# Attention heads of a hybrid trunk layer: pool waits by tile, two more side blocks ahead of the first value products, query weights converted behind the last head

## The chip, the core and the metric

The kernel runs on one core of a Trainium2 chip. The metric is the device time of one execution in microseconds (us); a kernel is run several times and the median stands for it. The core's engines are TensorE (PE in the profile, its weight loads PEld), VectorE (DVE), ScalarE (ACT), GpSimd (POOL) and SyncE (SP), whose queue issues nearly all DMAs. Each engine takes its instructions in a fixed order and waits on semaphores of the others.

## The reference

One layer of 1024 tokens and width 1024: a mixer of two head groups (forgetting attention, "fox", and gated linear attention), cross-attention to 256 memory tokens, and a squared-ReLU MLP.

```python
def fox_attention(q, k, v, log_f):
    c = jnp.transpose(jnp.cumsum(log_f, axis=1), (0, 2, 1))
    for i in range(S // Q_BLOCK):                      # 8 blocks of 128 queries, keys up to their end
        s = jnp.einsum('bqhd,bkhd->bhqk', qb, kb).astype(jnp.float32) * scale
        s = jnp.where(mask, s + c[:, :, start:end, None] - c[:, :, None, :end], -jnp.inf)
        p = jax.nn.softmax(s, axis=-1)
        outs.append(jnp.einsum('bhqk,bkhd->bqhd', p.astype(vb.dtype), vb))

def parallel_mixer(xn, ...):
    proj = xn @ w_in                                   # both mixers' inputs
    fox_out = fox_attention(rms_norm(fq), rms_norm(fk), fv, log_sigmoid(ff + b))   # 8 heads of 64
    gla_out = rms_norm(gla_chunked(gq, gk, gv, g_log)) * silu(gr)                  # 4 heads
    return concatenate([fox_out, gla_out], axis=-1) @ w_out

def memory_cross_attention(hn, memn, ...):             # 4 heads of 256, 256 memory tokens
    q = rms_norm(hn @ wq); k, v = split(memn @ wkv); k = rms_norm(k)
    return softmax(q k^T / 16) v @ wo

h = x + parallel_mixer(rms_norm(x), ...)
h = h + memory_cross_attention(rms_norm(h), rms_norm(mem), ...)
y = h + relu(rms_norm(h) @ w1)**2 @ w2                 # 1024 -> 4096 -> 1024
```

## The kernel before

All matrices are float32. A large product splits both operands into a rounded high part and a low rest, of type float32r, and makes three matmuls of each pair of tiles (high x high, low x high, high x low): `gemm`, L110 to L112. Every operand so needs a high part from ACT (a copy that rounds: `wh`, `sh`, `pth`) and a low part from DVE (`wl`, `sl`, `ptl`: the source less the high part). `wsplit` (L80 the load `raw`, L88 or L99 the high part, L93 or L100 the low part) does it for weights, `split_half` (L843, L844) for activations, `evac_split` (L117, L118, or L120, L121 with a factor) for what comes out of PSUM.

The stages follow each other: projections and linear attention, then `fox`, `project_out`, cross-attention, `project_o`, and the MLP. This case lies in `fox`, 324 to 548 us after the span's start, and at its end. There are 8 heads. For each, two groups g of four score tiles t (`fox_scores`): PE makes the scores (`s`, L660 to L663, 128 queries x up to 1024 keys), DVE the negated maximum (`nm`, L665), ACT the exponential with its row sum (`p`, L668), DVE the reciprocal (`rrec`, L670) and POOL scales (L671). Scores of more than 512 keys take a wide PSUM tile `s2`, of which there is one, the others an `s1`, also one. `values` then takes two of these tiles at a time (sub-block sb of four): PE transposes (`tr`, L696), ACT and DVE split the result into `pth` and `ptl`, PE multiplies by the values (`pv`, L704, of `va`), ACT copies half of the sum (`ol`, L707), DVE adds the other half (`mixf`, L710). The tiles of the first group of head 0 have their scores made ahead of `fox`. The values reach `va` by way of DRAM: the stage before stores `vd` (L600), `fox` loads it per head (L723).

So that PE has work while the softmax runs, a generator `side_work` gives independent products in blocks: eight blocks of `out_part` 0 (12 matmuls each, the linear attention's share of the mixer's output, `mm`, with `t2k` for the sum with x), then keys and values of the memory (`wkv`, `memr`, 24 matmuls each), then eight blocks of `out_part` 1 (18 each). `step` says after which of the 32 sub-blocks the next block is written:

```python
            def step(s):
                for _ in range(((s + 1) * 26 + 8) // 32 - (s * 26 + 8) // 32):
                    next(side, None)
```

The order in the program is not the order of the code: a scheduler, which works with estimated times of its own, chooses for each engine what comes next among what is ready. `issue_after(x)` holds it: what is issued inside goes behind the instruction x. For heads 6 and 7 the side blocks are held behind the first transposes.

SBUF is given out by pools that are opened and closed like a stack. A new pool over the memory of an old one waits: by default every first use of its tiles waits for all of the old pool's users, with `reuse_waits="tile"` for the users of the memory under that tile alone. `foxpt` holds `pth` and `ptl`, five of each, `foxol` holds `ol`, three. Both lie where the stage before had its tiles, among them those that the stores `vd` read.

Cross-attention converts its query weights (`wq`, `weights(n)`: `wh` L99, `wl` L100) as early as buffers allow, and the first of them are made during the last head.

## Time and profile before

| | |
|---|---|
| median of 3 runs | 1440.09 us (1438.77 to 1441.18) |
| profiled execution | 1440.62 us, its span 1438.9 us |
| PE busy | 1421.3 us, 99% of the span |
| DVE, ACT, POOL busy | 937.8, 675.2, 385.2 us |
| TensorE clock, mean | 0.998 of full |

The times are of runs of the same program; the profile is one execution, 0.53 us above their median. The span runs from its first instruction to its last; 1.7 us of the execution lie outside it. Busy shares are means over stages with different limits, so the prediction reads the stretch in which the change lies.

### The profile page before, as it was taken

The numbers are of one execution on the slowest core, as the hardware profiler recorded it, in microseconds if no ns is written. First come the engines' busy times: TensorE is split into PE (matmuls) and PEld (weight loads), VectorE is DVE, ScalarE is ACT, GpSimd is POOL, SyncE is SP. The second block draws the span as 40 slices with busy tenths as digits, with TensorE's granted clock in tenths as the row PEclk, the third lists the DMA queues.
The fourth block names the chain that finished last, engine by engine and source line by source line (L and its number), as shares of the span: only waits on it lengthen the run. The fifth ranks groups of instructions, "written<-read, shape, count | busy, mean of one in ns | idle before, by whom it ended". The sixth has DMA issues, their size and how long they took to land.

```text
span 1438.9 us, 19147 instructions
## 1 busy us (share of the span) xinstructions
PE 1421.3 (99%) x7036; PEld 1185.4 (82%) x7036; DVE 937.8 (65%) x1342; ACT 675.2 (47%) x1095; POOL 385.2 (27%) x404
## 2 busy tenths in 40 slices
PE   9999999999999999999999999999999999999998
PEld 7788788887888887888888888888888888888887
DVE  5366732437887766666545895656556968778797
ACT  3544441336777655454532364444546745335230
POOL 3235423311333223412212300000000552233454
PEclk9999999999999999999999999999999999999999
DMA  8335530278678634322573124344446835436353
GB/s 313 92 65 140 130 79 0 74 190 285 173 193 239 177 110 148 124 74 90 171 273 140 44 95 179 145 168 190 176 175 231 320 107 190 134 133 217 123 191 124
DMA packets 121164, 223.91 MB, mean 156 GB/s; under 512 B 8912, under 2 KB 54512, under 8 KB 118512
## 3 DMA queue, kind: packets, MB, share of 16 engines
q1 hardware_dynamic: 119776, 218.25, 46.6%
q10 hardware_dynamic: 1296, 4.46, 1.0%
q8 instruction: 55, 0.90, 0.2%
q14 instruction: 37, 0.30, 0.1%
HBM read 150.59 MB, written 72.09 MB: 155 GB/s over the span
## 4 chain that ended last, share of the span: by engine, by line
PE 89%; DMA 4%; ACT 3%; DVE 2%; issue 2%; POOL 0%; SPq 0%; ACTq 0%; DVEq 0%; POOLq 0%
PE mm L110 15%; PE mm L111 15%; PE mm L112 15%; PE my L110 7%; PE my L112 7%; PE my L111 7%; PE tr L112 3%; PE tr L111 3%; PE tr L110 3%; PE pv L704 2%; PE tr L696 2%; PE s L660 1%; PE s L661 1%; DMA ud<-h 1%; DMA raw<-in_mlp_w_dram 1%
## 5 line engine op out<-in xcount | busy, mean ns | idle before, releaser
L110 PE MATMUL my<-x,g 128*128 128x512 f32 x464 | 180.7, 390 | 0.5 <-ACT h L1295 0.3
L111 PE MATMUL my<-x,g 128*128 128x512 f32 x464 | 180.6, 389 | 0.0
L112 PE MATMUL my<-x,g 128*128 128x512 f32 x464 | 180.5, 389 | 0.0
L111 PE MATMUL mm<-wl,xh 128*128 128x512 f32 x320 | 126.5, 396 | 0.6 <-DVE wl L100 0.6
L110 PE MATMUL mm<-wh,xh 128*128 128x512 f32 x320 | 125.9, 396 | 0.5 <-ACT wh L99 0.4
L112 PE MATMUL mm<-wh,xl 128*128 128x512 f32 x320 | 125.7, 393 | 0.0
L1087 ACT ACTIVATE g<-s 128x1024 fp32r<-128x1024 f32 (+1 forms) x72 | 69.0, 964 | 101.1 <-PE my L112 41.1
L1088 DVE TENSOR_TENSOR g<-raw,g 128x512 fp32r<-128x512 f32 (+3 forms) x72 | 69.2, 965 | 69.8 <-ACT g L1087 69.7
L1087 ACT ACTIVATE g<-raw 128x512 fp32r<-128x512 f32 (+3 forms) x72 | 55.5, 773 | 102.4 <-DMA raw<-in_mlp_w_dram 39.6
L110 PEld LDWEIGHTS my<-x,g 128*128 128x128 f32 x464 | 87.1, 188 | 19.5 <-ACT h L1295 0.7
L111 PEld LDWEIGHTS my<-x,g 128*128 128x128 f32 x464 | 87.1, 188 | 18.3 <-DVE x L1088 0.2
L1114 POOL TENSOR_TENSOR s<-raw 128x384 f32<-128x384 f32 (+1 forms) x20 | 26.5, 1324 | 282.1 <-DMA raw<-in_mlp_w_dram 254.5
L112 PEld LDWEIGHTS my<-x,g 128*128 128x128 f32 x464 | 87.1, 188 | 17.9
L671 POOL TENSOR_SCALAR p<-p,rrec 128x128 f32<-128x128 f32 (+3 forms) x64 | 52.8, 831 | 151.6 <-DVE rrec L670 143.1
L1088 DVE TENSOR_TENSOR g<-s,g 128x1024 fp32r<-128x1024 f32 (+1 forms) x72 | 86.6, 1205 | 9.0 <-ACT g L1087 9.0
L1257 DVE TENSOR_TENSOR x<-x 128x1024 fp32r<-128x1024 f32 (+1 forms) x64 | 77.0, 1223 | 17.6 <-ACT x L1256 17.3
L111 PE MATMUL mm<-x,g 128*128 128x512 f32 x220 | 85.7, 389 | 0.0
L110 PE MATMUL mm<-x,g 128*128 128x512 f32 x220 | 85.6, 389 | 0.0
L112 PE MATMUL mm<-x,g 128*128 128x512 f32 x220 | 85.6, 389 | 0.0
L110 PE MATMUL tr<-x,g 128*128 128x512 f32 x212 | 82.5, 389 | 0.0
L111 PE MATMUL tr<-x,g 128*128 128x512 f32 x212 | 82.5, 389 | 0.0
L112 PE MATMUL tr<-x,g 128*128 128x512 f32 x212 | 82.5, 389 | 0.0
(316 smaller groups left out, 3665.8 us busy)
## 6 DMA issues: line engine op xcount, KB each, us to landing
ud<-h SPq DMA_DIRECT2D x32, 768.0 KB
x<-ud SPq DMA_DIRECT2D x48, 512.0 KB
raw<-in_mlp_w_dram SPq DMA_DIRECT2D x20, 1024.0 KB
raw<-in_mlp_w_dram SPq DMA_DIRECT2D x16, 768.0 KB
raw<-in_w_in_dram SPq DMA_DIRECT2D x23, 512.0 KB
raw<-in_xattn_wkv_dram SPq DMA_DIRECT2D x16, 512.0 KB
od<-o SPq DMA_DIRECT2D x32, 256.0 KB
ud<-h SPq DMA_DIRECT2D x32, 256.0 KB
```

The costliest lines, as they stand in the source:

```text
L110: mm(ps, lh[k], rh[k], start=start and k == 0, stop=False, **kw)
L111: mm(ps, lh[k], rl[k], start=False, stop=False, **kw)
L112: mm(ps, ll[k], rh[k], start=False, stop=stop and k == n - 1, **kw)
L660: nc.tensor.matmul(ps[:, c], qa[:, ts], ka[:, c], start=True, stop=False)
L661: nc.tensor.matmul(ps[:, c], qb[0:68, ts], kb[0:68, c], start=False, stop=not last)
L671: nc.gpsimd.tensor_scalar(p[:, 0:n], p[:, 0:n], rr, 1.0, ALU.mult, ALU.mult)
L696: t = nc.tensor.transpose(tp[:, c * P:(c + 1) * P], pp[i][:, (2 * b + j) * P:(2 * b + j + 1) * P], self.ident)
L704: nc.tensor.matmul(pv[:, 256 - (js.stop - js.start):256], va[:, 2 * b + j, :], w[:, js], start=b == j == 0 and w is th, stop=b == sb and j ...
L1087: a = self.nc.scalar.activation(hi, src, AF.Copy)
L1088: d = self.nc.vector.tensor_tensor(lo, src, f(hi), ALU.subtract)
L1114: eng.tensor_tensor(s[:, 0], raw[:, 3], raw[:, 2], ALU.add)
L1257: nc.vector.tensor_tensor(lo, f(lo), f(hi), ALU.subtract)
```

## The change

Three parts. The pool `foxpt` is opened behind `foxol` and waits by tile. Three side blocks are written ahead of the heads instead of one, the steps spread 24 instead of 26 blocks over the sub-blocks, and the first value products (head 0, sub-block 0) are held behind the last matmul of the third side block. The conversions of the query weights are held behind the last head's last two instructions. In the changed kernel the lines of `fox` stand one higher up to the value products and four to six higher behind them.

```diff
     def gemm(...):
...
-            mm(ps, ll[k], rh[k], start=False, stop=stop and k == n - 1, **kw)
+            end = mm(ps, ll[k], rh[k], start=False, stop=stop and k == n - 1, **kw)
+        return end.ins
...
     def fox(self):
-            pt = self.open(st, "foxpt", 5)
             olp = self.open(st, "foxol", 3)
+            pt = self.open(st, "foxpt", 5, reuse_waits="tile")
...
-                    for j, w in ((0, th), (1, th), (1, tl), (0, tl)):
-                        js = slice(j * 256, min((j + 1) * 256, n * P))
-                        nc.tensor.matmul(pv[...], va[:, 2 * b + j, :], w[:, js], ...)
+                    with ExitStack() as behind:
+                        if h == sb == 0:
+                            behind.enter_context(self.tc.issue_after(self.side_end))
+                        for j, w in ((0, th), (1, th), (1, tl), (0, tl)):
+                            js = slice(j * 256, min((j + 1) * 256, n * P))
+                            nc.tensor.matmul(pv[...], va[:, 2 * b + j, :], w[:, js], ...)
...
-                nc.scalar.activation(ol, pv[64:128, :], AF.Copy)
+                end = nc.scalar.activation(ol, pv[64:128, :], AF.Copy).ins
...
-                nc.vector.tensor_tensor(o, v3(pv[0:64, :]), v3(ol), ALU.add)
+                self.fox_end = end, nc.vector.tensor_tensor(o, v3(pv[0:64, :]), v3(ol), ALU.add).ins
...
-            next(side)
+            for _ in range(3):
+                next(side)
...
-                for _ in range(((s + 1) * 26 + 8) // 32 - (s * 26 + 8) // 32):
+                for _ in range(((s + 1) * 24 + 8) // 32 - (s * 24 + 8) // 32):
                     next(side, None)
...
     def out_part(...):
-                self.gemm(ps, *([w[:, c] for w in w_] for w_ in W), *A)
+                self.side_end = self.gemm(ps, *([w[:, c] for w in w_] for w_ in W), *A)
...
             def weights(n):
-                Ws[n] = self.wsplit(self.wq[:, n * 512:(n + 1) * 512], C_XAT)
+                with self.tc.issue_after(self.fox_end[0]), self.tc.issue_after(self.fox_end[1]):
+                    Ws[n] = self.wsplit(self.wq[:, n * 512:(n + 1) * 512], C_XAT)
```

The scheduler makes another order of it. Five places show what the prediction counts on. A number behind a name is that of the tile; the numbers of the two programs differ.

ACT, head 0, first conversions and the exp (`p`) of its last tile, before:

```order
L668 ACTIVATE p_550_2952,rsum_2953<-s_548_2944,nm_2950 128x896 [waits DVE_49]
L117 ACTIVATE pth_2862<-tr_2858 128x384 [waits DMAHW6_49,PE_49,DMAHW7_49,Activation_49,Pool_49]
L117 ACTIVATE pth_2896<-tr_2891 128x512 [waits PE_49]
L117 ACTIVATE pth_2909<-tr_2904 128x512 [waits PE_49]
L668 ACTIVATE p_555_2964,rsum_2965<-s_553_2958,nm_2962 128x512 [waits DVE_49,Pool_49]
L117 ACTIVATE pth_2921<-tr_2917 128x384 [waits PE_49]
L88 ACTIVATE wh_3738<-raw_783_3736 128x512 [waits DMAHW1_49]
L88 ACTIVATE wh_3742<-raw_783_3736 128x512
L88 ACTIVATE wh_3748<-raw_3746 128x512 [waits DMAHW0_49]
L88 ACTIVATE wh_3752<-raw_3746 128x512
L668 ACTIVATE p_560_2978,rsum_2979<-s_558_2970,nm_2976 128x1024 [waits DVE_49,Pool_49]
```

and now:

```order
L669 ACTIVATE p_554_2986,rsum_2987<-s_552_2978,nm_2984 128x896 [waits DVE_49]
L118 ACTIVATE pth_2896<-tr_2892 128x384 [waits PE_49,Activation_49,Pool_49]
L118 ACTIVATE pth_2930<-tr_2925 128x512 [waits PE_49]
L118 ACTIVATE pth_2943<-tr_2938 128x512 [waits PE_49]
L669 ACTIVATE p_559_2998,rsum_2999<-s_557_2992,nm_2996 128x512 [waits DVE_49,Pool_49]
L118 ACTIVATE pth_2955<-tr_2951 128x384 [waits PE_49]
L88 ACTIVATE wh_3683<-raw_769_3681 128x512 [waits DMAHW1_49]
L88 ACTIVATE wh_3687<-raw_769_3681 128x512
L88 ACTIVATE wh_3693<-raw_3691 128x512 [waits DMAHW0_49]
L88 ACTIVATE wh_3697<-raw_3691 128x512
L669 ACTIVATE p_564_3012,rsum_3013<-s_562_3004,nm_3010 128x1024 [waits DVE_49,Pool_49]
```

The row pth_2862, now pth_2896, has lost its two waits on DMAs; the rest keeps its order, with the four wh ahead of the exp.

PE at the same place, from the transposes of head 0 on, before (s_594 is head 1's first wide score):

```order
L696 MATMUL tr_2985<-ident_75,p_555_2964 128x128 [waits Pool_49]
L696 MATMUL tr_2985<-ident_75,p_545_2938 128x128
L696 MATMUL tr_2985<-ident_75,p_555_2964 128x128
L696 MATMUL tr_2998<-ident_75,p_555_2964 128x128 x2
L704 MATMUL pv_2857<-pth_2862,va_2426 128x256 [waits DMAHW7_49,DMAHW6_49,DMAHW3_49]
L704 MATMUL pv_2857<-pth_2862,va_2426 128x128
L704 MATMUL pv_2857<-ptl_2863,va_2426 128x128
L704 MATMUL pv_2857<-ptl_2863,va_2426 128x256
L660 MATMUL s_594_3115<-ka_2848,qa_2846 128x512 [waits Activation_49]
L661 MATMUL s_594_3115<-kb_2849,qb_2847 128x512
```

and now (s_606 is that score):

```order
L697 MATMUL tr_3019<-ident_75,p_559_2998 128x128 [waits Pool_49]
L697 MATMUL tr_3019<-ident_75,p_549_2972 128x128
L697 MATMUL tr_3019<-ident_75,p_559_2998 128x128
L697 MATMUL tr_3032<-ident_75,p_559_2998 128x128 x2
L661 MATMUL s_606_3165<-ka_2882,qa_2880 128x512 [waits Activation_49]
L662 MATMUL s_606_3165<-kb_2883,qb_2881 128x512
L661 MATMUL s_606_3165<-ka_2882,qa_2880 128x256
L662 MATMUL s_606_3165<-kb_2883,qb_2881 128x256
L664 LDWEIGHTS identb_93
L664 MATMUL s_606_3165<-maskb_98,identb_93 128x128
```

The four value products that stood ahead of the score have gone behind it and behind the third side block.

ACT at the fourth side block, before:

```order
L117 ACTIVATE pth_3036<-tr_3031 128x512 [waits PE_49,Activation_49]
L117 ACTIVATE pth_3049<-tr_3044 128x512 [waits PE_49,Activation_49]
L117 ACTIVATE pth_3062<-tr_3057 128x512 [waits PE_49,Activation_49]
L707 ACTIVATE ol_2929<-pv_2890 64x256 [waits PE_49]
L843 ACTIVATE sh_3191<-mixg_120 128x512 [waits PE_49]
L843 ACTIVATE sh_3195<-mixg_120 128x512 [waits PE_49]
L120 ACTIVATE sh_3568<-memr_3576,cols_74 128x256 [waits DMAHW7_49,PE_49]
L120 ACTIVATE sh_3568<-memr_3576,cols_74 128x256
```

and now:

```order
L711 ACTIVATE ol_2904<-pv_2891 64x256 [waits DMAHW7_49,DMAHW6_49,PE_49]
L849 ACTIVATE sh_3055<-mixg_120 128x512 [waits PE_49]
L849 ACTIVATE sh_3059<-mixg_120 128x512 [waits PE_49]
L121 ACTIVATE sh_3445<-memr_3453,cols_74 128x256 [waits DMAHW7_49,PE_49]
L121 ACTIVATE sh_3445<-memr_3453,cols_74 128x256
L121 ACTIVATE sh_3446<-memr_3453,cols_74 128x256 [waits PE_49]
L121 ACTIVATE sh_3446<-memr_3453,cols_74 128x256
L118 ACTIVATE pth_3086<-tr_3081 128x512 [waits PE_49,Activation_49]
L118 ACTIVATE pth_3099<-tr_3094 128x512 [waits PE_49,Activation_49]
L711 ACTIVATE ol_2963<-pv_2924 64x256 [waits PE_49]
```

Two sh and four conversions of memr have moved ahead of pth_3086 and pth_3099.

DVE in the last head (nm_5645 is the maximum of a tile of 1024 keys, rrec_5636 the reciprocal of the tile before it), before:

```order
L118 TENSOR_TENSOR ptl_5568<-tr_5563,pth_5567 128x384 [waits DVE_49,Activation_49]
L670 RECIPROCAL rrec_5636<-rsum_5634 128x1 [waits Activation_49]
L710 TENSOR_TENSOR mixf_2772<-pv_5520,ol_5533 64x2x128 [waits Activation_49]
L817 TENSOR_TENSOR t2k_5597<-mm_5578,t2k_5597 128x512 [waits DMAHW7_49,DMAHW2_49,PE_49]
L665 TENSOR_REDUCE nm_5645<-s_1345_5639 128x1 [waits PE_49]
L670 RECIPROCAL rrec_5650<-rsum_5648 128x1 [waits Activation_49]
```

and now:

```order
L119 TENSOR_TENSOR ptl_5579<-tr_5573,pth_5578 128x512 [waits DVE_49,Activation_49]
L119 TENSOR_TENSOR ptl_5591<-tr_5586,pth_5590 128x384 [waits DVE_49,Activation_49]
L666 TENSOR_REDUCE nm_5645<-s_1345_5639 128x1 [waits PE_49]
L671 RECIPROCAL rrec_5636<-rsum_5634 128x1 [waits Activation_49]
L714 TENSOR_TENSOR mixf_2772<-pv_5559,ol_5598 64x2x128 [waits Activation_49]
L671 RECIPROCAL rrec_5650<-rsum_5648 128x1 [waits Activation_49]
```

The reciprocal has gone behind the wide maximum, and two ptl ahead of it.

DVE behind the last side block, before:

```order
L118 TENSOR_TENSOR ptl_5725<-tr_5719,pth_5724 128x512 [waits DVE_49,Activation_49]
L710 TENSOR_TENSOR mixf_2772<-pv_5653,ol_5679 64x2x128 [waits Activation_49]
L100 SCALAR_TENSOR_TENSOR wl_6155<-raw_6152,cols_74,wh_6154 128x512 [waits DMAHW7_49,Activation_49]
L100 SCALAR_TENSOR_TENSOR wl_6159<-raw_6152,cols_74,wh_6158 128x512 [waits Activation_49]
L118 TENSOR_TENSOR ptl_5738<-tr_5732,pth_5737 128x512 [waits DVE_49,Activation_49]
L118 TENSOR_TENSOR ptl_5750<-tr_5745,pth_5749 128x384 [waits Activation_49]
L844 TENSOR_TENSOR sl_5829<-mixf_2772,sh_5828 128x512 [waits Activation_49]
L844 TENSOR_TENSOR sl_5969<-mixf_2772,sh_5968 128x512 [waits Activation_49]
L844 TENSOR_TENSOR sl_5973<-mixf_2772,sh_5972 128x512 [waits Activation_49]
```

and now:

```order
L119 TENSOR_TENSOR ptl_5725<-tr_5719,pth_5724 128x512 [waits DVE_49,Activation_49]
L119 TENSOR_TENSOR ptl_5738<-tr_5732,pth_5737 128x512 [waits DVE_49,Activation_49]
L850 TENSOR_TENSOR sl_5829<-mixf_2772,sh_5828 128x512 [waits Activation_49]
L850 TENSOR_TENSOR sl_5969<-mixf_2772,sh_5968 128x512 [waits Activation_49]
L850 TENSOR_TENSOR sl_5973<-mixf_2772,sh_5972 128x512 [waits Activation_49]
L119 TENSOR_TENSOR ptl_5750<-tr_5745,pth_5749 128x384 [waits Activation_49]
L714 TENSOR_TENSOR mixf_2772<-pv_5705,ol_5757 64x2x128 [waits Activation_49]
L100 SCALAR_TENSOR_TENSOR wl_6155<-raw_6152,cols_74,wh_6154 128x512 [waits DMAHW7_49,Activation_49]
L100 SCALAR_TENSOR_TENSOR wl_6159<-raw_6152,cols_74,wh_6158 128x512 [waits Activation_49]
```

The two wl of the query weights have gone behind the heads' last rows, and three sl have come ahead of ptl_5750.

More of the change, by code (lines that the diff above doesn't have):

```diff
@@ L701, in values @@
                     self.evac_split(th[:, 0:n * P], tl[:, 0:n * P], tp[:, 0:n * P])
-                    for j, w in ((0, th), (1, th), (1, tl), (0, tl)):
-                        js = slice(j * 256, min((j + 1) * 256, n * P))
-                        nc.tensor.matmul(pv[:, 256 - (js.stop - js.start):256], va[:, 2 * b + j, :], w[:, js],
-                                         start=b == j == 0 and w is th, stop=b == sb and j == 0 and w is tl)
+                    with ExitStack() as behind:
[3 more added lines that the diff above has]
+                            js = slice(j * 256, min((j + 1) * 256, n * P))
+                            nc.tensor.matmul(pv[:, 256 - (js.stop - js.start):256], va[:, 2 * b + j, :], w[:, js],
+                                             start=b == j == 0 and w is th, stop=b == sb and j == 0 and w is tl)
                 ol = self.T(olp, [64, 256], F32, "ol")
-                nc.scalar.activation(ol, pv[64:128, :], AF.Copy)
+                end = nc.scalar.activation(ol, pv[64:128, :], AF.Copy).ins
                 o = self.mixf[(h % 2) * 64:(h % 2) * 64 + 64, 2 * sb:2 * sb + 2, h // 2, :]
                 v3 = lambda ap: ap.rearrange("p (a b) -> p a b", a=2)
-                nc.vector.tensor_tensor(o, v3(pv[0:64, :]), v3(ol), ALU.add)
+                self.fox_end = end, nc.vector.tensor_tensor(o, v3(pv[0:64, :]), v3(ol), ALU.add).ins
                 return first
```

## The prediction

> **What bounds the kernel now.** I read the page's busy shares first, then TensorE's waits over the whole span, then the clock by stretches, then the order of time around the places where the change moves rows.
>
> ```profile
> span 1438.9 us, 19147 instructions
> PE 1421.3 (99%) x7036; PEld 1185.4 (82%) x7036; DVE 937.8 (65%) x1342; ACT 675.2 (47%) x1095; POOL 385.2 (27%) x404
> PE tr L696 <- DVE ptl L118: 4.5, 2, 3.2
> 332.00:336.00 4.00, 1.11 (x4) 0.74 (x5) 1.90 (x4) 2.42 (x6) 0.00 (x0) 0.71 1.04 399
> 336.00:340.00 4.00, 4.00 (x12) 3.23 (x13) 4.00 (x8) 3.02 (x6) 0.69 (x1) 0.50 1.03 387
> 340.00:344.00 4.00, 4.00 (x26) 3.42 (x26) 2.77 (x7) 2.69 (x8) 1.04 (x1) 0.93 1.06 256
> ```
>
> PE is idle for 1438.9 - 1421.3 = 17.6 us in all, so no edit of the order can bring more than that and what half clock costs. The third row is a line of the waits (total, times, longest): one wait of 3.2 us is the longest of the attention heads. The last three rows are stretches of 4 us (behind PE, PEld, ACT, DVE and POOL the sixth figure is the granted clock): 0.71, 0.50, 0.93. At half clock for the shares .29, .50 and .07 doubled, that is 2.3 + 4.0 + .6 = 6.9 us.
>
> ```profile
> 328.41 1.58 SPq L80 DMA_DIRECT2D raw<-in_xattn_wkv_dram  x2
> 330.15 0.67 DVE L665 TENSOR_REDUCE nm<-s 128x1 f32<-128x512 f32 x1
> 331.33 0.23 PE L663 MATMUL s<-maskb,identb 128*128 128x128 bf16 x1
> 333.57 1.47 ACT L117 ACTIVATE pth<-tr 128x384 fp32r<-128x384 f32 x3 [4.31 <-DMA vd<-qn]
> 334.10 1.18 DVE L118 TENSOR_TENSOR ptl<-tr,pth 128x384 fp32r<-128x384 f32 x2 [3.28 <-ACT pth L117]
> 334.80 0.87 PE L696 MATMUL tr<-ident,p 128*128 128x128 f32 x3 [3.24 <-DVE ptl L118]
> 337.18 2.19 ACT L88 ACTIVATE wh<-raw 128x512 fp32r<-128x512 f32 x4 [0.98 <-DMA raw<-in_xattn_wkv_dram]
> 339.27 1.10 ACT L668 ACTIVATE p<-s,nm 128x1024 f32<-128x1024 f32 x1
> 341.24 0.93 PE L696 MATMUL tr<-ident,p 128*128 128x128 f32 x7
> 341.92 0.43 PE L704 MATMUL pv<-pth,va 128*128 128x256 f32 x2
> 342.46 0.40 PE L660 MATMUL s<-ka,qa 128*128 128x512 f32 x1
> 343.57 0.47 PE L110 MATMUL mm<-sh,wh 128*128 128x512 f32 x1
> 346.42 0.49 PE L696 MATMUL tr<-ident,p 128*128 128x128 f32 x3
> ```
>
> These rows are in order of time (start, length). ACT's first conversion of weights (pth) stood idle 4.31 us for the last store of the values (vd), DVE's ptl stood behind it, and PE's next transposes behind ptl: nothing from 331.56 to 334.80. Every one of these tiles comes out of the pool foxpt, which waited for all of the old one.
>
> **Place A, the first head: +0.9 us.** With the pool by tile the order keeps neither wait on the DMA. nm ends at 330.82, pth is done by then, and ptl takes 0.6 (1.18 / 2), so PE goes straight on at 331.56. That frees 3.24 us, and with it the half clock that followed: PE works at half from 334.80 to 340.54, which costs 5.74 / 2 = 2.87.
>
> What is late next: PE does the second side block's rest, a block of 12 matmuls takes 346.42 - 343.57 = 2.85 and seven transposes about 0.7, and is through by 336.3. The next row is the score of head 1, and it needs the wide bank that ACT's exp of head 0's last tile empties. In ACT's order that exp stands behind the four wh, and these behind the load of raw, issued at 328.41, which let the first start at 337.18. Neither changes. So exp runs from 339.27 to 340.37 as before, and PE waits from 336.3 to 340.4, 4.1 us. Before, PE had already more to do there and came to this score at 342.46, when exp was long over. Now it starts it 2.1 earlier, but the first value products (341.92 to 342.46, 0.54) are still owed: 1.5 ahead.
>
> A wait of 3.24 was followed by half clock from 2.15 us after its start, for 6.9 us. Put on a wait that starts at 336.3, this is 338.45 to 345.3, of which PE works 4.9 and loses 2.4. Ends: 0 if the clock holds, 3.0 if the half rate sets in a microsecond later. A wait longer than one that was punished is nearest to that one, so I take 2.4: 2.4 - 1.5 = +0.9, with ends -1.5 and +1.5.
>
> The Trainium skill, "TensorE: Matmul & The Clock Gate", section "Part 1: The HAM clock gate (the "warmup" mystery)", says that the clock halves after an idle window of about 3.4 us and comes back after about 3.4 us of sustained work. The trace has the halving after less idling than that, and 5.74 us of work before the full clock. By the Trainium skill's rule this term would be 1.7 - 1.5 = +0.2.
>
> **Place B, the fourth side block: +0.75.**
>
> ```profile
> 348.77 0.48 PE L704 MATMUL pv<-pth,va 128*128 128x256 f32 x2
> 349.35 1.58 ACT L117 ACTIVATE pth<-tr 128x512 fp32r<-128x512 f32 x3 [3.65 <-PE pv L704]
> 349.98 1.88 DVE L118 TENSOR_TENSOR ptl<-tr,pth 128x512 fp32r<-128x512 f32 x3 [0.81 <-PE pv L704]
> 350.27 0.40 PE L110 MATMUL mm<-sh,wh 128*128 128x512 f32 x1
> 351.24 1.25 ACT L843 ACTIVATE sh<-mixg 128x512 fp32r<-128x512 f32 x2
> 351.78 0.40 DVE L710 TENSOR_TENSOR mixf<-pv,ol 64x256 f32<-64x256 f32 x1
> 352.53 1.71 ACT L120 ACTIVATE sh<-memr,cols 128x256 fp32r<-128x256 f32 x4
> ```
>
> Before, ACT made three pth and ol ahead of the sh of the second half. Now two sh, which wait for the block's first and second three matmuls to give their buffers back, and four conversions of memr stand ahead of pth_3086 and pth_3099. Count from the block's start: the second sh can start at 6/12 of 2.85 = 1.4 and ends at 2.05 (1.25 / 2 each), the memr rows (1.71) at 3.75, pth_3086 (1.58 / 3) at 4.3, its ptl (1.88 / 3) at 4.9; the second pair's ptl at 5.5. PE is through the block at 2.85; the twelve value products of the second sub-block (348.77 to 350.27, 1.5) and four transposes (0.4) bring it to 4.75. With 0.1 for a hand-over (ptl ends at 334.10 + 0.59, PE starts at 334.80) it waits 0.25 for the first ptl, three transposes later 0.3 for the second, and I add 0.2, half a mixf, for the bank of the next value products. Ends: 0 (the rows fit into the slack) and 1.25 + 1.71 = 2.96 (none does).
>
> **Place C, heads 6 and 7: +2.6.**
>
> ```profile
> 504.00:540.00 36.00, 35.27 (x212) 29.81 (x212) 24.48 (x49) 19.91 (x46) 9.34 (x11) 1.00 0.33 110
> 523.18 0.48 POOL L671 TENSOR_SCALAR p<-p,rrec 128x256 f32<-128x256 f32 x1 [5.27 <-DVE rrec L670]
> 523.98 0.96 DVE L665 TENSOR_REDUCE nm<-s 128x1 f32<-128x768 f32 x1 [0.90 <-PE s L663]
> 525.46 0.50 PE L704 MATMUL pv<-ptl,va 128*128 128x128 f32 x2 [0.45 <-DVE ptl L118]
> 534.80 1.22 DVE L665 TENSOR_REDUCE nm<-s 128x1 f32<-128x1024 f32 x1 [0.43 <-PE s L663]
> 537.36 0.17 DVE L670 RECIPROCAL rrec<-rsum 128x1 f32<-128x1 f32 x1 [1.33 <-ACT p L668]
> 337.76 0.69 POOL L671 TENSOR_SCALAR p<-p,rrec 128x512 f32<-128x512 f32 x1 [5.93 <-DVE rrec L670]
> ```
>
> Before, PE idles 36.00 - 35.27 = 0.73 there. Two side blocks that were spread over the heads are gone to the front, so fewer matmuls lie between a score and the transposes that use it, and at three places the narrow tile's rrec now stands behind the wide tile's nm on DVE. At tr_5654 the path is nm 1.22 + rrec 0.17 + POOL 0.69 + three hand-overs of about 0.1 = 2.4, against PE work of eight value products (0.54 / 4 each by 341.92 to 342.46) and two transposes, 1.2, or only the last three of these, 0.3, since the last ptl (0.6) stands ahead of nm too: a wait of 1.2 to 2.1, I take 1.5. At tr_5314 the same 2.4 and a ptl, 3.0, meet twelve products, three transposes and a narrow score, some 2.3: 0.7. At tr_5521 nm 0.96 + 0.17 + POOL 0.48 + 0.3 = 1.9 meets four products, three transposes and a narrow score, some 1.2: 0.7. One short wait for ptl like that of 525.46 is 0.4. Sum 3.3, less 0.73. Ends: -0.7 (all covered, old waits too) and +3.2 (2.1 at tr_5654).
>
> **Place D, behind the last side block: -0.6.**
>
> ```profile
> 540.00:544.00 4.00, 3.19 (x24) 2.77 (x22) 4.00 (x8) 3.32 (x7) 0.00 (x0) 1.00 0.52 184
> 544.00:548.00 4.00, 2.62 (x17) 2.13 (x18) 3.94 (x8) 3.47 (x7) 0.00 (x0) 1.00 0.49 152
> 543.67 1.28 DVE L118 TENSOR_TENSOR ptl<-tr,pth 128x512 fp32r<-128x512 f32 x2
> 545.43 1.41 DVE L100 SCALAR_TENSOR_TENSOR wl<-raw,cols,wh 128x512 fp32r<-128x512 f32 x2
> 546.76 1.15 DVE L118 TENSOR_TENSOR ptl<-tr,pth 128x512 fp32r<-128x512 f32 x2
> 547.49 0.51 PE L704 MATMUL pv<-ptl,va 128*128 128x256 f32 x2 [0.47 <-DVE ptl L118]
> 547.82 1.88 DVE L844 TENSOR_TENSOR sl<-mixf,sh 128x512 fp32r<-128x512 f32 x3
> ```
>
> PE idles 0.81 + 1.38 = 2.2 here. Two wl (1.41) leave DVE's way to ptl_5738 and ptl_5750, and three sl (1.88), which are not held, move ahead of ptl_5750, the last one. The first of the two ptl comes 1.4 sooner, the last 1.88 - 1.41 = 0.5 later; the value products that close the head need both, but PE has the first one's done by then, and the rows of 543.67 to 547.49 have PE waiting for every ptl. I take -0.6, between -1.4 and +0.5. The wl come after the heads, where DVE's sl stood, beside project_out's first products.
>
> **The heads between (345 to 504)** are reordered with no place that stands out: 0, ends -1.5 and +1.5. The SP queue issues the same loads in the same order up to the stores of t2k, so no DMA is priced. The two loads of the query weights keep their place; their buffers come free later, where the DMA engines are half idle (0.49 in the last of the two stretches).
>
> **The sum.** The profiled execution took 1440.62, 0.53 over the median of 1440.09. 1440.62 + 0.9 + 0.75 + 2.6 - 0.6 = 1444.3, and 0.53 less as a median: 1443.7, +0.25%. A measurement of this kernel tells about 0.2% (2.9 us) from no change: 1437.2 to 1443.0 is "same".
>
> **The rivals.**
> 1. The wait at A goes and none follows: the wkv loads land before 334 or so, so that the four wh are done and exp is over by 336.3. Then A is -3.24 - 2.87 = -6.1 instead of +0.9: 1443.7 - 7.0 = 1436.7. For it: the page's wait list has only this long one. Against: wh started at 337.18, at once when raw had landed, and the issue at 328.41 hangs on nothing that moves; it must come 3 us sooner. 0.16, faster.
> 2. Heads 6 and 7 hide their rows: C is 0, 1441.1. For it: before, rows of the same form cost 0.73 there in 36 us. 0.21, same.
> 3. The second wait at A is not followed by half clock, or for a shorter time: 1443.7 - 2.4 = 1441.3. For it: one wait is one observation, and where the halving starts within a wait is not known. By the Trainium skill's rule, named above, with one window of work at half, the time would be 1443.0. 0.10, same.
> 4. The edit of the query weights does not clear DVE: three sl take the room of two wl and all of the 0.5 is on the path: 1443.7 + 0.6 + 0.5 = 1444.8. 0.10, slower.
>
> **How the numbers follow.** The forecast has 0.43, of which 0.03 falls below 1443.0 by the spread of the middle heads. Faster 0.16; same 0.21 + 0.10 + 0.03 = 0.34; slower 0.40 + 0.10 = 0.50. Range: down to rival 1, a little below it 1436.5; up to 1443.7 with A at +1.5, C at +3.2 and the middle heads at +1.5, which is 1446.4, and 1 us more for B: 1447.5. The forecast's own range is 1442 to 1446.5.
>
> **What would show it.** PE tr has no wait for ptl at 331.6; PE s L661 waits some 4 us for ACT's p at 336 to 340.4, with the granted clock near 0.5 behind it. If instead the row of wh starts before 335, rival 1 has it. In 500 to 540 the waits of tr for POOL p add up to about 3; if they stay under 1, rival 2. In 540 to 548 PE idles about 1.6. The forecast is wrong if the score of head 1 starts before 337, or if the middle heads gain more than 1.5.

## The result and the profile after

The changed kernel took 1451.26 us (median of 4 runs, 1450.25 to 1452.21) against 1440.18 of the kernel before (4 runs beside it): ratio 1.008, interval 1.0067 to 1.0093. It is slower by 11 us, where 3.5 us were predicted (1443.7, range up to 1447.5): the sign was right, the size was not. The profiled execution took 1451.27 us, so it stands for the median; its span is 10.6 us longer than that of before.

The page of after, then its TensorE waits from 324 to 560 us (total, times, longest):

```profile
span 1449.5 us, 19157 instructions
PE 1424.4 (98%) x7036; PEld 1186.9 (82%) x7036; DVE 940.5 (65%) x1342; ACT 675.3 (47%) x1095; POOL 388.1 (27%) x404
...
PE tr L697 <- POOL p L672: 5.9, 5, 3.1
PE s L661 <- ACT p L669: 4.1, 2, 3.9
PE tr L697 <- DVE ptl L119: 1.8, 3, 0.9
PE pv L708 <- DVE ptl L119: 1.5, 3, 1.1
```

The wait for ptl has shrunk from 4.5 us before (its line stands in the prediction) to 1.8. Two others have grown; before, they were:

```profile
PE tr L696 <- POOL p L671: 1.1, 1, 1.1
PE s L660 <- ACT p L668: 0.3, 1, 0.3
```

The wait of the score behind ACT's exp was predicted. Of the waits of the transposes behind POOL's scaling, one alone is 3.1 us, and that one was not. Stretches of after (busy time of PE, PEld, DVE, ACT, POOL, then granted clock, DMA share, GB/s), and last the third of them as it was before:

```profile
336.00:340.00 4.00, 0.63 (x3) 0.53 (x4) 3.23 (x7) 3.96 (x9) 0.00 (x0) 1.00 1.05 374
340.00:344.00 4.00, 4.00 (x15) 3.23 (x14) 2.74 (x6) 2.13 (x6) 2.33 (x4) 0.58 0.98 254
460.00:504.00 44.00, 39.99 (x250) 34.20 (x249) 30.27 (x63) 25.26 (x59) 14.65 (x14) 0.96 0.58 160
504.00:540.00 36.00, 33.52 (x199) 28.23 (x198) 22.94 (x44) 17.16 (x41) 6.76 (x10) 1.00 0.37 117
540.00:544.00 4.00, 3.75 (x25) 2.75 (x22) 3.68 (x7) 3.03 (x8) 1.02 (x1) 1.00 0.00 0
544.00:548.00 4.00, 2.90 (x16) 2.50 (x17) 2.46 (x7) 3.74 (x8) 1.82 (x2) 1.00 0.00 0
```
```profile
460.00:504.00 44.00, 43.76 (x268) 37.01 (x266) 34.39 (x68) 29.86 (x67) 9.68 (x12) 1.00 0.61 179
```

From 460 to 504 PE idled 0.24 us before and 4.01 after, at full clock before and at 0.96 after, while POOL's busy time grew from 9.68 to 14.65 with two instructions more.

To say where the 11 us arose, the two traces are compared at equal work: each form of matmul counts its median spacing between starts, and what counts is when each program has reached the same sum. The table counts the spacing ahead of each matmul. The orders differ, so a single figure is good to about 1 us: with the spacing behind each matmul the middle heads come to +4.3 and place C to +4.6.

| stretch (times of before) | later by | predicted |
|---|---|---|
| before 324 (same order in both) | -0.8 | |
| 324 to 344, place A | -0.6 | +0.9 |
| 344 to 360, place B | +1.6 | +0.75 |
| 360 to 462, middle heads | -0.6 | 0 |
| 462 to 466, middle heads, one place | +4.8 | 0 |
| 466 to 490, middle heads | +1.0 | 0 |
| 490 to 540, place C | +3.5 | +2.6 |
| 540 to 550, place D | -0.4 | -0.6 |
| 550 to 600, first products behind the heads | +1.1 | 0 |
| 600 to the end | +1.0 | 0 |

The place of the +4.8, on DVE, POOL and PE of after:

```profile
458.44 0.14 DVE L671 RECIPROCAL rrec<-rsum 128x1 f32<-128x1 f32 x1
458.51 0.67 DVE L93 TENSOR_TENSOR wl<-raw,wh 128x512 fp32r<-128x512 f32 x1
459.10 0.68 DVE L850 TENSOR_TENSOR sl<-mixg,sh 128x512 fp32r<-128x512 f32 x1
...
463.37 1.28 DVE L93 TENSOR_TENSOR wl<-raw,wh 128x512 fp32r<-128x512 f32 x2
464.58 0.41 DVE L714 TENSOR_TENSOR mixf<-pv,ol 64x256 f32<-64x256 f32 x1
```
```profile
458.68 6.54 POOL L672 TENSOR_SCALAR p<-p,rrec 128x512 f32<-128x512 f32 x1 [4.54 <-DVE rrec L671]
```
```profile
465.27 0.77 PE L697 MATMUL tr<-ident,p 128*128 128x128 f32 x5 [3.15 <-POOL p L672]
```

The scaling of the same tile (head 4, 512 keys) before:

```profile
450.13 0.70 POOL L671 TENSOR_SCALAR p<-p,rrec 128x512 f32<-128x512 f32 x1
```

After, it takes 6.54 us instead of 0.70, from 458.68 to 465.22, while DVE makes ten conversions in a row that read and write SBUF (only a reciprocal between; the fence leaves six rows out). It ends 0.57 us after the last of the ten (464.65), when a mixf, which reads PSUM, has begun. PE stands 3.15 us for it and then works at half clock for 3.41 us from 466.9.

### The profile page after: what moved, and what is told of

The parts are those of the page before. It is cut to its first block, busy times and chain, and to the rows that moved or that the text cites. A ratio compares the mean times of both kernels' runs of the same rounds, so it can differ in the third digit from the quotient of the medians.

```text
span 1449.5 us, 19157 instructions
## 1 busy us (share of the span) xinstructions
PE 1424.4 (98%) x7036; PEld 1186.9 (82%) x7036; DVE 940.5 (65%) x1342; ACT 675.3 (47%) x1095; POOL 388.1 (27%) x404
## 4 chain that ended last, share of the span: by engine, by line
PE 87%; DMA 4%; DVE 3%; ACT 3%; issue 2%; POOL 1%; SPq 0%; ACTq 0%; DVEq 0%; POOLq 0%
PE mm L110 15%; PE mm L111 14%; PE mm L112 14%; PE my L110 7%; PE my L111 7%; PE my L112 7%; PE tr L111 4%; PE tr L112 4%; PE tr L110 4%; PE pv L708 2%; PE tr L697 1%; DMA raw<-in_xattn_wkv_dram 1%; PE s L661 1%; PE s L662 1%; POOL p L672 1%
## 5 line engine op out<-in xcount | busy, mean ns | idle before, releaser
L672 POOL TENSOR_SCALAR p<-p,rrec 128x128 f32<-128x128 f32 (+3 forms) x64 | 57.6, 905 | 163.8 <-DVE rrec L671 162.9
```

What stands on the lines that cost most here:

```text
L672: nc.gpsimd.tensor_scalar(p[:, 0:n], p[:, 0:n], rr, 1.0, ALU.mult, ALU.mult)
```

## The experiments

Every ratio is against the kernel before, run beside it on the same chip. A profile is one execution, and what is read of it holds for that one: it lies within 2.4 us of its kernel's median, but 2.7 above it in after_dve_scale, 3.9 in steps_24_only and 5.2 in exp_first_act_scale. The first three take the change apart.

**pool_only**: the pool by tile alone; all else as before.

> Before with the pool by tile alone (one side block ahead, 26 steps, query weights free): no engine's order of instructions changes, only the wait of pth on the stores goes. Theory A (the DMA of the values is late anyway): PE goes straight on at 331.6, does the second side block and then stands before the first value products for the load of va, which landed at 339.8 before, some 3.6 us, with half clock behind it; the time stays within 3 us of before, 1438 to 1442. Rival (the wait on the stores was all): nothing follows and the time falls by 6, to 1434.

Measured 1.0017 (1.0005 to 1.0029). PE's row after the first transposes:

```profile
339.81 0.68 PE L705 MATMUL pv<-pth,va 128*128 128x256 f32 x2 [2.99 <-DMA va<-vd]
```

The wait is not gone but has moved to the first value products, which need va, and va is loaded from what the same stores write. Half clock follows for 6.83 us from 339.9. So the pool's wait was cover for the load, and the hold of the first value products is what answers it.

**side_only**: three blocks ahead, the hold and 24 steps; pool and query weights as before.

> Before with the three side blocks ahead, 24 steps and the first value products held, but the pool and the query weights as before. Theory P (the cost lies at the block of conversions that the new steps put on DVE at 458 to 465, ten in a row, beside POOL's scaling of p, and in heads 6 and 7): most of the 11 us of the changed kernel are here too, 1447 to 1450, with a wait of tr for POOL of about 3 us near 462 and half clock behind it. Rival (the cost hangs on the pool or the query weights): 1440 to 1443.

Measured 1.0071 (1.0054 to 1.0089). PE's waits from 324 to 560:

```profile
PE tr L697 <- POOL p L672: 5.8, 5, 2.8
PE tr L697 <- DVE ptl L119: 3.4, 4, 1.6
PE pv L708 <- DVE mixf L714: 2.3, 1, 2.3
```

Nearly the whole loss is in this part, with the 6.54 us scaling again. The wait of 2.3 us for mixf, which ends at 554.19, is not in after. Here ACT makes two conversions of the query weights ahead of the ol that mixf needs, the first of which waits 1.36 us for its load; in after these stand behind the heads.

**wq_only**: the hold of the query weights alone.

> Before with the query weights' conversions behind the last head alone; some ten rows an engine move, all behind the last side block. Theory of the prediction: PE idles 0.6 less in 540 to 548, 1439.5. Rival (three sl take the room of two wl): 0.5 to 1.5 more, 1441 to 1442.

Measured 0.9995 (0.9986 to 1.0004): same. The 0.47 us wait for ptl at 547 is gone, and PE idles 1.7 us from 540 to 550 where it idled 2.2; but in the profiled execution 3.41 us of half clock follow from 545.9, which the profile of before does not have.

**Is it the slow scaling?** Two kernels move it off POOL.

```diff
+AS = ((4, 3), (4, 7))          # after_dve_scale: nc.vector for (4, 3) alone
...
-        nc.gpsimd.tensor_scalar(p[:, 0:n], p[:, 0:n], rr, 1.0, ALU.mult, ALU.mult)
+        if (h, t) in AS:
+            nc.scalar.activation(p[:, 0:n], p[:, 0:n], AF.Identity, scale=rr)
+        else:
+            nc.gpsimd.tensor_scalar(p[:, 0:n], p[:, 0:n], rr, 1.0, ALU.mult, ALU.mult)
```

> The changed kernel with one of POOL's 64 scalings, that of head 4's tile of 512 keys near 458.7, given to DVE. Theory P (POOL can't get at its operands while DVE works through conversions that read both operands from SBUF: 6.54 us for a scaling that takes 0.7 elsewhere): the wait of 3.15 us near 462 goes and the half clock of 3.4 us behind it, 1446 to 1447. Rival (the wait comes from the order of PE's rows, and another takes its place): 1450 to 1452.

Measured 1.0096 (1.008 to 1.0111). The next scaling on POOL (1024 keys, at 467.5) then took 3.42 us and PE waited 2.23 for it, and other rows moved. It separates nothing.

> The changed kernel with both scalings of head 4 that meet DVE's run of conversions near 458 to 468 (512 and 1024 keys) given to ACT, so that POOL has nothing to do beside it; the run stays eight long. Theory P: the wait of 3.15 us for POOL and the half clock of 3.4 us behind it go, in all 4.8, 1446 to 1447.5, if heads 6 and 7 keep their waits. Rival (PE waits there for the conversions themselves, as it did for mm in two of the runs before): 1449 to 1452.

Measured 1.0078 (1.0063 to 1.0093), with two of head 4's scalings (512 and 1024 keys) on ACT. At the place itself it did what it should: the wait for POOL is gone, a shorter one is left, and at equal work 462 to 466 costs 1.2 instead of 4.8 us.

```profile
465.64 0.50 PE L111 MATMUL mm<-sh,wh 128*128 128x512 f32 x1 [1.18 <-ACT t2k L787]
...
509.00 0.80 PE L712 MATMUL pv<-pth,va 128*128 128x256 f32 x2 [1.91 <-DVE mixf L718]
```

But the order behind it is another one: a wait of 1.91 us for mixf with 6.83 us of half clock, and more to the end of the heads, made it 10.4 late at 550, where after is 8.5 late. So the slow scaling is the direct cause of some 3.6 of the 4.8 there. Taking it away does not bring the time back, because the new order loses elsewhere.

**after_rrec_first** tests place C: in heads 6 and 7 the wide maximum is held behind the previous reciprocal.

```diff
+        with ExitStack() as behind:
+            if h >= 6 and t >= 4:
+                behind.enter_context(self.tc.issue_after(self.rrec))
             nc.vector.tensor_reduce(nm, ps[:, 0:n], AX.X, ALU.max, negate=True)
...
+        self.rrec = nc.vector.reciprocal(rr, rs).ins
```

> The changed kernel with DVE's wide maxima of heads 6 and 7 held behind the reciprocal of the tile before. Theory of the prediction at place C: the waits of tr for POOL in 504 to 550 (2.5 us in the changed kernel) go down to about 1, 1449 to 1450. Rival (the maximum comes later and the next tile's exp, scaling and transposes with it): 1451 to 1453.

Measured 1.0075 (1.0059 to 1.0092). The first fence is after from 504 to 560, the second this kernel:

```profile
PE tr L697 <- POOL p L672: 2.5, 3, 1.1
```
```profile
PE tr L700 <- POOL p L675: 0.7, 2, 0.5
PE pv L711 <- DVE mixf L717: 1.2, 2, 0.8
```

The reciprocal behind the maximum does make the waits for POOL, as the prediction said. Of the 1.8 us won, waits for mixf took 1.2, and the time is not told from after's 1.0080.

**Is it the number of steps?** 22 steps instead of 24, and the first conversions `wh` of the memory weights (a quarter of them) held behind the exp of head 0's last tile; then both.

```diff
-                for _ in range(((s + 1) * 24 + 8) // 32 - (s * 24 + 8) // 32):
+                for _ in range(((s + 1) * 22 + 8) // 32 - (s * 22 + 8) // 32):
```
```diff
+                        if self.hold is not None:      # exp_end for the first quarter of wkv
+                            behind.enter_context(self.tc.issue_after(self.hold))
                         self.wsplit_hi = nc.scalar.activation(wh, r, AF.Copy).ins
...
+        if (h, t) == (0, 7):
+            self.exp_end = end
```

after_22_steps and exp_first_22 also lack the hold of the first value products, which their expectations do not mention.

> The changed kernel with 22 instead of 24 in the formula of the steps, so that DVE's conversions for the last eight side blocks are spread (no run longer than six ahead of the last head). Theory P: POOL has no scaling over 2 us, the wait of tr for POOL near 462 and its half clock go, 1445 to 1448. Rival (any order with three blocks ahead loses as much in other waits): 1449 to 1453.

Measured 1.0069 (1.0053 to 1.0085). The slow scaling near 460 is gone, and the kernel is as slow. In its place PE waits 3.1 us for va (the hold is missing) and 3.0 us at 460.6 for a t2k of ACT, each with 6.83 us of half clock. The time is the rival's. As the hold is missing too, it is not shown what 22 steps alone would cost; most of the loss arose far behind the hold, around the wait for t2k (0.7 us ahead at 440, 6.5 late at 490).

> The changed kernel with ACT's first conversions of wkv held behind the exp of head 0's last tile. Place A of the prediction: PE's wait of 3.9 us at 335.5 and the half clock behind it (1.7 lost) go, a short wait for va at most is left, so 1445 to 1447 if all else stays; the run of conversions on DVE is still nine long. Rival (the wait only turns into one for va, which lands at about 339.8): 1450 to 1452.

Measured 1.0031 (1.0019 to 1.0043). Place A came out with the gain that the prediction's first rival named, though by another way: at equal work -5.5 from 324 to 344, since exp no longer stands behind the loads. The slow scaling at 458 did not occur either, and at 504 the kernel was still 4.1 ahead. Then a wait of 1.94 for mixf at 502.4 with half clock, and 3.5 us in six shorter waits from 533 to 552 with half clock twice, gave back 10. The profiled execution is one of the longer ones, 1447.25 against a median of 1445.03.

> Both of these edits on the changed kernel. If both theories hold and the gains add, 1439 to 1442, beside before at 1440; under both rivals 1449 to 1453.

Measured 1.0064 (1.0042 to 1.0087), slower than the one edit alone: a scaling of 256 columns took 3.57 us, and PE waited 3.0 of it.

> The changed kernel with both: the conversions of wkv behind the exp, and the two scalings on ACT. The gain of place A (about 4 us by position of PE against the changed kernel) and no wait for POOL near 462: 1441 to 1445, the rest being heads 6 and 7 and the end. Rival (a new order brings other waits of the same size): 1446 to 1450.

Measured 1.0071 (1.0043 to 1.0099), both edits together. The rival held here too: waits for mixf (3.2 in two), for a t2k of DVE (2.3) and one of ACT (2.2).

**The steps alone, and everything but the steps.**

```diff
 # steps_24_only: before, with
-                for _ in range(((s + 1) * 26 + 8) // 32 - (s * 26 + 8) // 32):
+                for _ in range(((s + 1) * 24 + 8) // 32 - (s * 24 + 8) // 32):
 # steps_as_before: pool, three blocks ahead and hold of after; no query weights' hold; and
+                for _ in range(max(2, ((s + 1) * 26 + 8) // 32) - max(2, (s * 26 + 8) // 32)):
```

In steps_as_before no block is written until before's count has caught up, so that only 46 rows of PE and 18 of DVE stand elsewhere than before.

> Before with 24 instead of 26 in the formula of the steps and nothing else. Theory S: the later heads lose as in the changed kernel, 1444 to 1449, with a wait of 1 us or more for POOL or for a late conversion between 400 and 560. Rival (it takes the blocks ahead and the hold too): 1439 to 1442.

Measured 1.0095 (1.0077 to 1.0114): this one number makes at least as large a loss as the whole change (1.0080, 1.0067 to 1.0093). At equal work it is 3.3 late at 462 and 10.9 at 466, by another mechanism than after's. ACT, then PE:

```profile
463.76 0.38 ACT L708 ACTIVATE ol<-pv 64x256 f32<-64x256 f32 x1 [0.50 <-PE pv L705]
470.37 0.63 ACT L118 ACTIVATE mkv<-t2k 128x512 fp32r<-128x512 f32 x1 [6.23 <-DMA kTd<-mkv]
471.02 1.08 ACT L118 ACTIVATE pth<-tr 128x512 fp32r<-128x512 f32 x2
```
```profile
471.68 0.79 PE L705 MATMUL pv<-pth,va 128*128 128x256 f32 x2 [4.47 <-ACT pth L118]
```

ACT's next row is the conversion of the memory's keys (mkv), which waits 6.23 us until the store kTd has read its buffer. pth stands behind it, and PE behind pth for 4.47, with 6.83 us of half clock from 471.5.

> Before with the pool by tile and the first value products held behind the third of three blocks written ahead, but then no block until the steps of before have caught up, so that from the fourth block on each is written where it was before (query weights as before). Only 46 rows of PE and 18 of DVE stand otherwise than before, nearly all in head 0. Theory S (the loss is in the order that 24 steps make of the later heads, not in the new wait of head 0): place A alone is left, 0.9 to 1.4 more than before, 1440 to 1442. Rival (the hold and the new wait cost the most): 1447 to 1451.

Measured 1.003 (1.0019 to 1.0042). The time lies between the two forecasts. From 360 to 545 it stays 1.0 late throughout, so the middle heads and heads 6 and 7 lose nothing when their order is kept. Places A and B cost 1.4 of it (-0.4 at 324 to 1.0 at 360). The rest came behind 545: half clock at 547 and 735, and a wait of 0.68 at 595. The waits ahead of the half clock at 547, 1.22 and 0.50 us, stand in before too, but there no half clock follows.

**With the exp freed, in the old order.** steps_as_before_exp adds the hold of `wh` behind exp, steps_as_before_exp_wq also that of the query weights.

> The kernel with the steps as before, and the conversions of wkv held behind the exp of head 0's last tile. The wait of place A goes (about 4 us by PE's position at the fourth block), and the later heads have nearly the steps of before: 1436 to 1438. Rival (the 525 rows of PE that stand otherwise bring waits of their own, as in the other kernels with that hold): 1439 to 1446.

Measured 1.002 (1.001 to 1.0029). At equal work it is 2.1 to 3.9 ahead from 360 to 540, and between 540 and 550 it loses some 4.5, at one place. ACT, then PE:

```profile
540.71 1.34 ACT L103 ACTIVATE wh<-raw,cols 128x512 fp32r<-128x512 f32 x2 [1.10 <-DMA raw<-in_xattn_wq_dram]
...
544.35 0.72 ACT L103 ACTIVATE wh<-raw,cols 128x512 fp32r<-128x512 f32 x1 [1.34 <-DMA raw<-in_xattn_wq_dram]
```
```profile
546.36 0.79 PE L714 MATMUL pv<-pth,va 128*128 128x256 f32 x2 [3.92 <-DVE mixf L720]
```

PE came earlier to the end of the heads, the query weights' load did not, and ACT waited for it ahead of the rows the heads needed.

> The kernel before this one (steps as before, conversions of wkv behind the exp) with the query weights' conversions held behind the last head too. In its profile ACT stood in the last head with two conversions of the query weights ahead of ol, the second load landing late, and PE waited 3.92 us at 542.4 for the mixf behind it, with half clock after it. Theory: this wait and its half clock (up to 3.4) go, and what place A won stays: 1435 to 1438, under before. Rival (DVE's sl or another wait takes the room): 1440 to 1443.

Measured 1.0003 (0.9992 to 1.0013), the same as before. The wait of 3.92 is gone, so here the third part of the change is worth some 2.4 us (1.0020 to 1.0003, good to about 2 us), where alone it was worth nothing that could be told. Its profiled execution is 1437.39 us, the shortest of its runs, and 2.6 ahead at 560; that does not stand for its median. The time lies above the forecast of 1435 to 1438, and no version is shown to beat the kernel before.

**What made the scaling slow?** Four kernels leave the layer out and time POOL's scaling beside runs of DVE or ACT work of one kind.

> A kernel that leaves the whole layer out and measures POOL's scaling of p by itself, in twelve phases: alone (512 and 1024 wide), and beside runs of DVE subtractions of 128x512 whose operands come both from SBUF (as for wl and sl), one from PSUM (as for ptl), or mixed, beside maxima from PSUM, and beside a run of scalar_tensor_tensor. Theory P: 0.7 us alone and beside subtractions or maxima from PSUM; beside twelve SBUF subtractions (about 7.5 us) it ends only when the run ends, 6 us or more, whatever its width; beside alternating ones somewhere between. Rival (POOL was slow for another reason): 0.7 to 1.5 us in every phase.

Alone, beside subtractions of two SBUF tiles, and beside subtractions with one operand in PSUM, as rows of POOL:

```profile
19.15 0.69 POOL L43 TENSOR_SCALAR p<-p,q 128x512 f32<-128x512 f32 x1 [12.27 <-DVE q L42]
...
22.23 1.51 POOL L43 TENSOR_SCALAR p<-p,q 128x512 f32<-128x512 f32 x1 [2.39 <-DVE q L42]
...
31.09 0.69 POOL L43 TENSOR_SCALAR p<-p,q 128x512 f32<-128x512 f32 x1 [7.35 <-DVE q L42]
```

So the two engines do contend where DVE has two SBUF operands, and by 0.8 us, not 5.9. The Trainium skill, "SBUF — State Buffer", section "Who interferes with whom", says that a DVE instruction with two SBUF inputs contends with a GpSimd one that reads SBUF, and that one with at most one SBUF input, outside the modes that use two ports, does not. Both halves agree with 1.51 against 0.69; the 6.54 it does not tell.

> A kernel that leaves the layer out and measures POOL's scaling of 128x512 beside a run of twelve SBUF subtractions on DVE, as the one before, but with the place of POOL's start within DVE's run moved from phase to phase by an operation of growing width between the reciprocal and the run (4 to 512 columns); then runs of three and six, and widths 256 and 1024. Theory P1 (whether POOL gets in hangs on the moment of its start): some phases take 1.2 to 1.9 us as in the kernel before this one, others 6 to 7, to the end of the run. Rival P2 (a run alone does not shut POOL out; in the changed kernel something else had to come with it): 1.2 to 1.9 in all.

Started inside an operation that reads PSUM, ahead of such a run: 0.69 at every offset.

> A kernel that leaves the layer out and measures POOL's scaling beside twelve SBUF subtractions on DVE, now with a first SBUF operation of growing width (16 to 496 columns) right behind the reciprocal, so that POOL starts at another place of DVE's run from phase to phase and always inside an operation that reads both operands from SBUF. Theory P1: in some phases POOL ends only with the run, 6 to 8 us; in others after 1.2 to 2. Rival P2: 0.7 to 2 in all of them.

Started inside an SBUF operation: from 0.69 rising steadily to 1.18 with the width of that operation. That is as if POOL waited until the running operation ends and got in ahead of the next.

> A kernel that leaves the layer out and measures POOL's scaling beside twelve SBUF subtractions on DVE whose second operand ACT has made, as wl's: in five phases all made ahead, in five more made beside the run, so that DVE's instructions wait for ACT; the start is moved by a first operation of 4 to 512 columns, and there are widths 256 and 1024. Theory P3 (POOL is shut out when DVE's next instruction stands ready behind a wait of its own): 3 us or more in phases of the second kind, 0.7 to 1.5 in the first. Rival: 0.7 to 1.5 in all, and the 6.54 us stay unexplained.

With the second operands made by ACT shortly ahead or meanwhile, as in the kernel: 0.69 to 1.18 in every phase of 512 columns. A scaling that stands through ten conversions was not reproduced. It was seen in after, side_only and after_rrec_first, which have the same order there, and in shorter form in seven others (2.40 to 3.57 us). In after_exp_first one of 256 columns (0.48 us by itself in scale_offsets) took 2.64 us beside five conversions and ended 0.35 us after the last of them, as that of after ended 0.57 us behind its ten. So in these places DVE kept POOL out for the whole run. At others POOL got in between two conversions of a run:

```profile
464.65 1.43 POOL L671 TENSOR_SCALAR p<-p,rrec 128x256 f32<-128x256 f32 x1 [2.04 <-DVE rrec L670]
```

This row is of before, beside four conversions, of which the last ends at 467.22. What decides between the two stays open.

## Why the prediction was right and wrong

**Place A** held in its mechanism: the wait for ptl went, and exp became the next late row.

```profile
336.04 2.19 ACT L88 ACTIVATE wh<-raw 128x512 fp32r<-128x512 f32 x4 [4.39 <-DMA raw<-in_xattn_wkv_dram]
338.13 1.09 ACT L669 ACTIVATE p<-s,nm 128x1024 f32<-128x1024 f32 x1
339.37 0.50 PE L661 MATMUL s<-ka,qa 128*128 128x512 f32 x1 [3.88 <-ACT p L669]
```

The wait is 3.88 (predicted 4.1). The half clock behind it lasted 3.41 us, half of what was carried over from before, and cost 1.7 instead of 2.4: A was -0.6, inside its ends of -1.5 and +1.5. A shorter half clock is what the third rival named. The first rival failed in this kernel by the row of 336.04; after_exp_first then won its 5.5 by moving the exp instead of the load.

**Place B** was +1.6 against +0.75, inside its ends. A and B together were predicted at +1.65 and measured +1.0.

**The middle heads** are the step that failed: "reordered with no place that stands out: 0, ends -1.5 and +1.5". They cost 5.2 us by the table: 5.8 from 462 to 490, less the 0.6 won ahead of it. The step looked at the new order for rows that move far. It did not look for what stands beside them: ten SBUF conversions in a row on DVE next to a scaling on POOL. The trace of before had a hint of it, the 1.43 us for 256 columns at 464.65 that is shown above. Even with that seen, the price would have been missed: the 6.54 us is not in the trace of before, and the small kernels give 1.5. The loss of some 5 us from 462 to 466 is the wait of 3.15 us and half of 3.41 us of half clock. steps_24_only shows the more general fault. Moving the steps reorders every later head, and each new order tried had some such place: POOL here, a store's buffer there, mixf, or t2k. steps_as_before, with the old order, has none from 360 to 545.

**Place C** was right in its mechanism and somewhat undersized: +3.5 against 2.6 by the table, just over its end of 3.2. PE idles 2.48 us from 504 to 540 and 1.35 from 540 to 548; these 3.83 less the 0.73 of before are 3.1. Its longer waits there:

```profile
512.49 0.30 PE L697 MATMUL tr<-ident,p 128*128 128x128 f32 x1 [0.90 <-DVE ptl L119]
516.37 0.77 PE L697 MATMUL tr<-ident,p 128*128 128x128 f32 x5 [0.93 <-POOL p L672]
533.08 0.44 PE L697 MATMUL tr<-ident,p 128*128 128x128 f32 x2 [0.43 <-POOL p L672]
545.10 0.77 PE L697 MATMUL tr<-ident,p 128*128 128x128 f32 x5 [1.13 <-POOL p L672]
```

The waits of tr for POOL are 2.5 us; the prediction named three of 1.5, 0.7 and 0.7. What it left out is the wait of tr for ptl, 0.90. The waits of pv for ptl, 0.45 in all, are what it allowed.

**Place D** was -0.4 against -0.6 by the table. PE idles 1.61 us from 548.9 to 558.5, the same work as 540 to 550 before, where it idled 2.19: 0.6 less. The last ptl, which three sl now precede, is the longest of these waits:

```profile
556.43 0.50 PE L708 MATMUL pv<-ptl,va 128*128 128x128 f32 x2 [1.06 <-DVE ptl L119]
```

**Behind 550** 2.1 us more were lost, 1.1 of them by 600, for which the prediction had no term. No run takes them apart.

The missing 7.8 us are then, by the table, the middle heads (+5.2), what lies behind 550 (+2.1), C (+0.9), B (+0.8), D (+0.2) and A (-1.5): 7.7. This sum starts at 324, where after stood 0.8 ahead by chance, so it is that much larger than the difference of the two spans.

## What to carry to other kernels

A change to how often side work is written is a change of every row behind it; price it by the new order, engine by engine, looking for conversions that wait for a DMA ahead of the rows the main path needs and for long runs of SBUF conversions on DVE beside a scaling on POOL, and give that term a wide, lopsided range. To learn what a single edit is worth, keep the rest of the order as it was, as steps_as_before does. When a stall is taken away, list all that the next rows wait for: here va, exp and the query weights each came into the light in turn, and three holds together only brought back the time of before.

## What the runs showed of the hardware

- Half clock came in lengths of 3.41 or 6.83 us, between 324 and 740 us in after and in every experiment of the layer but steps_as_before_exp_wq, which had none there. It came behind single waits of 1.26 us (at 541.16 in after_act_scale) to 4.47, and from 551.66 in after_exp_first behind three of 0.22, 0.50 and 0.69 us. The length does not follow the wait: 3.88 gave 3.41, 2.99 gave 6.83. Where it came, it cost up to another 1.7 or 3.4 us, half its length. The Trainium skill, "TensorE: Matmul & The Clock Gate", section "Part 1: The HAM clock gate (the "warmup" mystery)", has the clock halve after an idle window of about 3.4 us; in these traces less was enough.
- In each trace the starts of half clock lie whole multiples of 3.41 us apart (in after, 340.61 and 466.90 us are 37 of them apart). In the 3.41 us ahead of each of the 36 starts, PE idled at least 1.0 us in all. Of the stretches of 3.41 us between these multiples, from 30 to 1380 us, every one with more than 1.71 us of idling was followed by half clock; between 1.0 and 1.71 us it went either way. So where a wait falls decides too: waits of 1.22 and 0.50 us were followed by half clock in wq_only and steps_as_before and not in before.
- POOL's scaling of 128 x 512 took 0.69 us alone, 1.51 beside DVE work with two SBUF operands in a small kernel, and 6.54 in the kernel beside ten conversions in a row, until they were over; why POOL did not get in between them is not explained.
